# Delta-rule inverses: 32x32 blocks on VectorE, one doubling, substitution with two heads side by side

## The chip, the cores and the metric

The kernel runs on one core of one Trainium2 chip (the other cores are idle). The metric is the device time of one execution in microseconds; it is given as the median of several runs. Five engines work side by side, each through its own queue in order: TensorE (PE) multiplies, VectorE (DVE), ScalarE (ACT) and GpSimd (POOL) do elementwise work, SyncE (SP) issues most of the transfers. Here POOL issues transfers too.

## The reference, cut to what matters

One decoder layer on 256 tokens of width 2048, float32. A combined projection feeds branch A (gated DeltaNet, 8 heads of 128) and branch B (attention, 8 heads); both are gated, projected and added, then a gated MLP follows. The change is in the DeltaNet alone. Per head and chunk the reference computes

```python
a_mat = jnp.where(strict, jnp.einsum('bhncd,bhnsd->bhncs', kb, k) * gamma, 0.0)
t_mat = lax.linalg.triangular_solve(eye + a_mat, eye, left_side=True, lower=True, unit_diagonal=True)
u = jnp.einsum('bhncs,bhnsv->bhncv', t_mat, v * beta[..., None])
...
v_new = u_n - w_n @ state
o = qg_n @ state + qk_n @ v_new
state = state * gl_n + kd_n.T @ v_new
```

`gamma` holds the decays exp(gc[i] - gc[j]) between two tokens of a chunk. The kernel works in chunks of 128 tokens in place of 64, which is the same sum: per head it needs two strictly triangular 128x128 matrices A, the result (I + A)^-1 applied to the values, and the product of the second half's queries and keys with the first half's results.

## The kernel before, in words

**The main work.** Every large product runs as float32 split in a high and a low part, three matmuls of 128x128 by 128x256 for each 128x128 block of weights (`block`, L185 to L190, issued by `main_mm`, L110 to L115). Weights come by SP in 1 MB pieces; ACT rounds each piece to its high part `wh` and DVE subtracts for the low part `wl` (`split`, L120, L118), in halves of 1024 columns and with two buffers of each. The order of the program is: DeltaNet projections (four groups of two heads, each with q, k, v and the output gate z: `ps_gdn`, `ps_z`), attention projections (`ps_moba`, `ps_v`), branch gates (`ps_gate`), branch outputs, `ps_wo`, up (`ps_up`), down (`pd`).

**The background work.** DeltaNet and attention heads are Python generators in the list `bg`. `main_mm` counts 108 (or 215) for each main matmul and calls `tick` after every 1700 (`EVERY`, L29); `tick` advances each generator to its next `yield`, so a piece of background work is written into the program about every 16 main matmuls. `wait(n)` is n empty steps: main work that is put between a transfer and its use. Before the branch gates' tiles are allocated, the generators of the DeltaNet are run out (L702 to L704), since their buffers make room.

**What sets the order.** The program is compiled with a scheduler that runs a timeline model over it and orders each engine's instructions by it, with `tick`'s order as the priority. The order is fixed from then on: an instruction whose input is late holds all that stands behind it on its engine.

**One group's DeltaNet** (`gdn`, L453 to L605; a group is two heads, j, and two halves of 128 tokens, i, so four matrices A). `bc_g`: PE spreads the cumulated decays of a head to 128 partitions with a selecting matmul of their high and low part (L466 to L468). DVE and ACT make `gam` from it (L470 to L477). PE makes the products of keys and queries (`g0`, `g1`), DVE scales them to `aq0`, `aq1` (L506 to L510), which hold A transposed. A goes to DRAM (`dA`, L521, L522) and comes back as 32 diagonal blocks of 16x16, one for each partition (`Xa`, L524). DVE inverts these by 15 pairs of a product and a negated sum (`tm` L530, `X` L531). The blocks go to DRAM and back as `U`, four 128x128 matrices with 16x16 blocks on the diagonal (L537 to L539). Then three levels double the blocks to 32, 64 and 128 (L541 to L568): four transposes `t0`, four matmuls `py` with A, a mask on DVE, four matmuls `pu` with `U`, and a subtraction. With the whole inverse U, `u0` applies it to the first half's values, `r1` takes the first half's part off the second half, `u1` applies the second inverse (L570 to L583). `po` and what follows make the output.

**Queues at the change.** Its transfers are issued by POOL, in order with POOL's own work (squares `sqq` and `so`, rotary products of the attention L636, L637). Weights are issued by SP.

Of the kernel before, what the change touches and what calls it, by code (L numbers as in the profile page):

```python
# [11 lines left out]
F32 = mybir.dt.float32  # L12
F32R = mybir.dt.float32r
# [22 lines left out]
    ("ident", 128), ("nm", 128), ("my", 3 * 64), ("nm3", 3 * 128), ("invf", 1),  # L36
# [3 lines left out]
def const_array():  # L40
    c = {}
    i = np.arange(P)
    c["ident"] = np.eye(P)
    c["nm"] = np.where(i[None, :] >= i[:, None], 0.0, -30000.0)
    my = np.zeros((P, 3, 64))
    for j in range(3):
        m = 16 << j
        e = i[(i // m) % 2 == 0][None, :]
        my[:, j, :] = (i[:, None] // (2 * m) == e // (2 * m)) & ((i[:, None] // m) % 2 == 1)
    c["my"] = my  # L50
# [33 lines left out]
def layer_kernel(ctx: ExitStack, tc: tile.TileContext, xT, pos, cst, csel, ceye, vec, convw, ffw, bdv,  # L84
# [8 lines left out]
    def r3(t, b):  # L93
        return t.rearrange("p (a b) -> p a b", b=b)
# [221 lines left out]
    gch = fk.tile([16, T], F32R, name="gch")  # L316
    gcl = fk.tile([16, T], F32R, name="gcl")
    selr = fk.tile([16, 8, P], F32R, name="selr")
    dve.tensor_copy(selr, self_)
# [68 lines left out]
    def decay():  # L388
# [27 lines left out]
        split(gch, gcl, gc)  # L416
# [11 lines left out]
    def conv4(t, ps, b0):  # L428
# [8 lines left out]
        act.activation(t, t, AF.Silu)  # L437

    zero = fk.tile([P, P], F32, name="zero")
    pool.memset(zero, 0.0)  # L440

    dUs = []
    for i in range(2):
        dUs.append(dr.tile([4, P + 1, P], F32, name=f"dU{i}", bufs=1))

    def diag(d):
        return bass.AP(tensor=d.tensor, offset=d.offset, ap=[[16 * P + 16, 32], [P, 16], [1, 16]])
# [5 lines left out]
    def gdn(h0, kq, v):  # L453
        hs = (h0, h0 + 1)

# [13 lines left out]
        gam = g.tile([P, 2, 3, P], F32, name="gam", bufs=1)  # L469
        for j in range(2):  # L470
            c = 8 + hs[j]
            dve.scalar_tensor_tensor(gam[:, j, 0, :], pg[:, j, :P], cols[:, 0, c:c + 1], nm,
                                     op0=ALU.subtract, op1=ALU.min)
            dve.tensor_scalar(gam[:, j, 1, :], pg[:, j, P:], cols[:, 2, c:c + 1], 0.0, op0=ALU.add, op1=ALU.min)
            dve.scalar_tensor_tensor(gam[:, j, 2, :], pg[:, j, P:], cols[:, 1, c:c + 1], nm,
                                     op0=ALU.subtract, op1=ALU.min)
# [20 lines left out]
        act.activation(st[:, 2, :], st[:, 1, :], AF.Sqrt, bias=epst)  # L497
# [25 lines left out]
        Xa = g.tile([32, 16, 16], F32, name="Xa", bufs=1)  # L523
        pool.dma_start(Xa, diag(dA))  # L524
        X = g.tile([32, 16, 16], F32, name="X", bufs=1)
        pool.tensor_copy(X, eye)
        yield from wait(9)
        for i in range(1, 16):
            tm = g.tile([32, 16, 16], F32, name="tm", bufs=1)
            dve.tensor_tensor(tm[:, :i, :i], X[:, :i, :i], Xa[:, None, :i, i].to_broadcast([32, i, i]), op=ALU.mult)  # L530
            dve.tensor_reduce(X[:, :i, i], tm[:, :i, :i], axis=AX.X, op=ALU.add, negate=True)  # L531
            if i % 4 == 3:
                yield
        dU = dUs[h0 // 2 % 2]
        if h0 < 4:
            sp.dma_start(dU[:, :P].rearrange("p s c -> s p c"), zero[:, None, :].to_broadcast([P, 4, P]))
        pool.dma_start(diag(dU), X)  # L537
        U = g.tile([P, 4, P], F32, name="U0", tag="U", bufs=1)
        pool.dma_start(U, dU[:, :P].rearrange("p s c -> s p c"))  # L539
        yield from wait(12)  # L540
        for lv in range(3):  # L541
            w = 16 << lv

            def even(t):
                return t.rearrange("p a (b c d) -> p a b c d", c=2, d=w)[:, :, :, 0, :]

            def odd(t):
                return t.rearrange("p a (b c d) -> p a b c d", c=2, d=w)[:, :, :, 1, :]

            pst = r3(sdt("t0"), P)  # L550
            for p in range(4):
                pe.transpose(pst[:, p, :], U[:, p, :], ident)
            Tm = g.tile([P, 4, 64], F32, name="Tm", bufs=1)
            act.copy(Tm.rearrange("p a (b d) -> p a b d", d=w), even(pst))
            Y = g.tile([P, 4, P], F32, name="Y", bufs=1)
            pool.memset(odd(Y), 0.0)
            yield
            py = sdt("py")[:, :T].rearrange("p (a b) -> p a b", a=4)
            for p in range(4):
                pe.matmul(py[:, p], ats[p], Tm[:, p], start=True, stop=True)  # L560
            dve.tensor_tensor(even(Y), py.rearrange("p a (b d) -> p a b d", d=w),
                              my[:, lv:lv + 1, :].rearrange("p a (b d) -> p a b d", d=w).to_broadcast([P, 4, 64 // w, w]), op=ALU.mult)
            yield
            pu = sdt("pu")[:, :T].rearrange("p (a b) -> p a b", a=4)
            for p in range(4):
                pe.matmul(pu[:, p], Y[:, p, :], odd(U)[:, p], start=True, stop=True)  # L566
            dve.tensor_tensor(odd(U), odd(U), pu.rearrange("p a (b d) -> p a b d", d=w), op=ALU.subtract)
            yield  # L568
        u = g.tile([P, 4, P], F32, name="u", bufs=1)
        pu0 = r3(sdt("u0"), P)  # L570
        for j in range(2):
            pe.matmul(pu0[:, j, :], U[:, j, :], vb[:, j, :], start=True, stop=True)
        act.copy(u[:, 0:2, :], pu0[:, :2, :])
        yield
        pr = r3(sdt("r1"), P)
        for j in range(2):
            pe.matmul(pr[:, j, :], aq0[:, j, 0, P:], u[:, j, :], start=True, stop=True)
        dve.tensor_tensor(vb[:, 2:4, :], vb[:, 2:4, :], pr[:, :2, :], op=ALU.subtract)
        yield
        pu1 = r3(sdt("u1"), P)  # L580
        for j in range(2):
            pe.matmul(pu1[:, j, :], U[:, 2 + j, :], vb[:, 2 + j, :], start=True, stop=True)
        act.copy(u[:, 2:4, :], pu1[:, :2, :])  # L583
        yield
# [336 lines left out]
```

## Time and profile before

| | us |
|---|---|
| median of 3 runs | 1488.11 (1486.22 to 1488.19) |
| the profiled execution's own time | 1485.81 |
| its span, first to last instruction | 1484.0 |
| PE busy in the span | 1467.9 (99%) |
| DVE busy | 968.6 (65%) |
| ACT busy | 720.1 (49%) |
| POOL busy | 121.9 (8%) |

The DeltaNet's background work lies between about 60 and 410 us of the span; all after that is main work. In the groups and timelines a row names the line, the engine, the operation, output<-input, and the shape as partitions x elements. A float32 matmul appears twice, as two passes; a matmul of split operands and a transpose appear once. The duration of one PE row is longer than its share of PE's time, since matmuls overlap: what one costs is read from start to start.

### The profile page before, as it was taken

To read this page: it belongs to the slowest core of one execution; us is meant where nothing else is said; L and a number is where in the kernel's file an instruction comes from. 1 tells how busy PE (TensorE), PEld (TensorE's weight loads), DVE (VectorE), ACT (ScalarE), POOL (GpSimd) and SP (SyncE) were. 2 spreads that over 40 slices of the span, in tenths; PEclk is the share of its full clock that TensorE was granted. 3 is DMA by queue.
4 is the path that set the end of the run, shared out by engine and by line. 5 is a ranking of instruction groups with operands and counts; after the bars stand their busy time and mean duration, and the time that the engine had idled before them with its cause. 6 is when DMAs were issued, how large, how long until landed. Compare 5 with 4: busy or idle time off the path is not lost.

```text
span 1484.0 us, 26882 instructions
## 1 busy us (share of the span) xinstructions
PE 1467.9 (99%) x11472; PEld 1409.7 (95%) x11472; DVE 968.6 (65%) x1377; ACT 720.1 (49%) x949; POOL 121.9 (8%) x133
## 2 busy tenths in 40 slices
PE   9999999999999999999999999999999999999997
PEld 8999999998999999999999999999999998888886
DVE  7988695887665455766676666666666665445554
ACT  5655363434474344444455454554545554444444
POOL 0001101042121000110100000000000000000000
PEclk9999999999999999999999999999999999999999
DMA  9545544444436555557555555555555554555552
GB/s 335 178 165 180 179 151 161 147 161 155 143 114 226 184 191 195 198 200 277 186 193 199 195 188 191 195 199 199 187 190 194 198 200 170 197 189 189 193 197 86
DMA packets 43353, 277.23 MB, mean 187 GB/s; under 512 B 5248, under 2 KB 6736, under 8 KB 11104
## 3 DMA queue, kind: packets, MB, share of 16 engines
q1 hardware_dynamic: 41408, 270.98, 52.7%
q0 software_dynamic: 960, 2.36, 0.5%
q10 hardware_dynamic: 864, 2.16, 0.4%
q8 instruction: 90, 1.47, 0.4%
q14 instruction: 31, 0.25, 0.0%
HBM read 271.68 MB, written 3.80 MB: 186 GB/s over the span
## 4 chain that ended last, share of the span: by engine, by line
PE 91%; DVE 4%; DMA 2%; issue 1%; ACT 1%; SPq 0%; DVEq 0%; POOLq 0%; ACTq 0%
PE ps_up L111 32%; PE pd L99 16%; PE ps_gate L111 11%; PE ps_gdn L111 8%; PE ps_wo L111 6%; PE ps_br L111 6%; PE ps_moba L111 3%; PE ps_z L111 3%; PE ps_v L111 2%; DVE wl L118 1%; DMA wraw<-in_w_gdn 1%; ACT wh L121 1%; PE py L560 1%; PE g L99 0%; PE pu L566 0%
## 5 line engine op out<-in xcount | busy, mean ns | idle before, releaser
L118 DVE TENSOR_TENSOR wl<-wraw,wh 128x1024 fp32r<-128x1024 f32 (+1 forms) x500 | 605.7, 1248 | 199.7 <-ACT wh L121 199.3
L121 ACT CAST wh<-wraw 128x1024 fp32r<-128x1024 f32 (+1 forms) x500 | 496.1, 1040 | 464.8 <-PE ps_up L111 160.6
L111 PE MATMUL ps_up<-h,wh 128*128 128x256 f32 x2816 | 479.4, 276 | 0.0
L111 PEld LDWEIGHTS ps_up<-h,wh 128*128 128x128 f32 x2816 | 423.7, 188 | 0.1
L111 PE MATMUL ps_up<-h,wl 128*128 128x256 f32 x1408 | 388.9, 276 | 0.0
L111 PEld LDWEIGHTS ps_up<-h,wl 128*128 128x128 f32 x1408 | 264.3, 188 | 0.0
L111 PE MATMUL ps_gate<-hc,wh 128*128 128x256 f32 x1024 | 176.5, 277 | 0.0
L111 PEld LDWEIGHTS ps_gate<-hc,wh 128*128 128x128 f32 x1024 | 154.6, 188 | 0.0
L111 PE MATMUL ps_gate<-hc,wl 128*128 128x256 f32 x512 | 141.8, 277 | 0.4 <-DVE wl L118 0.4
L99 PE MATMUL pd<-wl,ah 128*128 128x512 f32 x336 | 130.9, 390 | 0.0
L99 PE MATMUL pd<-wh,al 128*128 128x512 f32 x336 | 130.8, 389 | 0.0
L111 PE MATMUL ps_gdn<-hc,wh 128*128 128x256 f32 x704 | 124.3, 280 | 0.0
L111 PEld LDWEIGHTS ps_gdn<-hc,wh 128*128 128x128 f32 x704 | 107.1, 188 | 0.8 <-ACT wh L121 0.3
L111 PE MATMUL ps_gdn<-hc,wl 128*128 128x256 f32 x352 | 98.7, 280 | 0.8 <-DVE wl L118 0.8
L111 PEld LDWEIGHTS ps_gate<-hc,wl 128*128 128x128 f32 x512 | 96.1, 188 | 0.6 <-DVE wl L118 0.6
L99 PE MATMUL pd<-wh,ah 128*128 128x512 f32 x336 | 92.8, 391 | 0.0
L111 PE MATMUL ps_moba<-hc,wh 128*128 128x256 f32 x512 | 92.6, 282 | 0.0
L211 DVE TENSOR_TENSOR unf<-ps_up,R 128x512 f32<-128x512 f32 x44 | 30.4, 691 | 88.9 <-PE ps_up L111 88.9
L111 PE MATMUL ps_wo<-mc,wh 128*128 128x256 f32 x512 | 87.1, 276 | 0.0
L111 PEld LDWEIGHTS ps_moba<-hc,wh 128*128 128x128 f32 x512 | 78.4, 189 | 0.2
L111 PEld LDWEIGHTS ps_wo<-mc,wh 128*128 128x128 f32 x512 | 77.2, 188 | 0.0
L121 ACT CAST ah<-acts 128x256 fp32r<-128x256 f32 x44 | 17.9, 407 | 119.2 <-PE pd L99 118.3
(429 smaller groups left out, 2001.9 us busy)
## 6 DMA issues: line engine op xcount, KB each, us to landing
wraw<-in_w_up SPq DMA_DIRECT2D x88, 1024.0 KB, 4.9
wraw<-in_w_dn SPq DMA_DIRECT2D x44, 1024.0 KB, 4.9
wraw<-in_w_gate SPq DMA_DIRECT2D x32, 1024.0 KB, 4.9
wraw<-in_w_gdn SPq DMA_DIRECT2D x30, 1024.0 KB, 4.9
wraw<-in_w_moba SPq DMA_DIRECT2D x16, 1024.0 KB, 4.9
wraw<-in_w_o SPq DMA_DIRECT2D x16, 1024.0 KB, 5.0
wraw<-in_w_mv SPq DMA_DIRECT2D x8, 1024.0 KB, 5.0
wraw<-in_w_ba SPq DMA_DIRECT2D x8, 1024.0 KB, 4.9
```

Of the source, the lines that this page charges most:

```text
L99: pe.matmul(ps, a, b, start=(start and i == 0), stop=(stop and i == n - 1), **kw)
L111: pe.matmul(ps, a, b, start=start, stop=stop, skip_group_check=True)
L118: return (eng or dve).tensor_tensor(lo, src, hi.bitcast(F32), op=ALU.subtract)
L121: act.copy(hi, src)
L211: dve.tensor_tensor(dst, ps, r, op=ALU.mult)
L560: pe.matmul(py[:, p], ats[p], Tm[:, p], start=True, stop=True)
```

## The change

**Decays.** The cumulated decays `gc` go to DRAM once (`dG`) and each group reads its two heads' rows back, spread over 128 partitions, straight into `gam`. The selecting matmuls and the split of `gc` go.

**32x32 inverses on DVE.** A goes to DRAM as before (`dA`). From there its sixteen 32x32 diagonal blocks are gathered (`dC`) and come back so that each block is held by eight partitions (`Xa`); each partition solves two rows of both 16x16 halves, again in 15 pairs of a product and a negated sum (shape 128 x 4 x i). The lower left 16x16 part follows on DVE by two small matrix products (`rows`, which makes `W` and then `Xm`); the second of them needs the lower block's inverse, which goes through DRAM (`dX`, `Xr`). The 32x32 inverses go to DRAM (`dE`), come back as `E`, and are also written on the diagonal of `UB`.

**One doubling for four blocks at once.** `Et` is a transpose of `E` in 32x32 pieces on DVE. One matmul `py` for each half i multiplies four blocks by their part of A (`S1`, block diagonal, read from `dA`); a mask (`Y`); one matmul `pu` for each i; ACT writes the negated result to `UB`.

**Substitution with two heads side by side.** `UB` holds 64x64 inverses of both heads on one diagonal. For each half i: `w0` applies the first, `z0` takes its part (`S2`, also from `dA`) off the values, `w1` applies the second. Values are laid out as two heads x 64 tokens (`v`, `vt`, `vb`, `rt2`); `apart` copies the results back to `u` in the order that `r1` and `po` read. The subtraction behind `r1` is four pieces.

The steps of a generator stay about as many: 47 yields before, 45 now, with other waits (10 before the inverses, 4 and 7 behind them).

**PE, where the first group's inverse is applied.** `t_..`, `py`, `pu` and `u_..` are the levels and the first application; `ps_gdn` is main work. Before, first level and the start of the second, up to the first application:

```order
L552 MATMUL t_1549<-ct,U_1236 128x128 x4
L111 MATMUL ps_gdn<-hc,wl 128x256
...
L560 MATMUL py<-Tm,aq_905 128x64 x2
L560 MATMUL py<-Tm,aq_906 128x64 x2
...
L566 MATMUL pu<-U_1236,Y 128x64 x4
...
L552 MATMUL t_1626<-ct,U_1236 128x128 x4
...
L566 MATMUL pu<-U_1236,Y 128x64 x4
...
L572 MATMUL u_1802<-vb,U_1236 128x128 x2
```

Now, the one doubling and the substitution of the first half:

```order
L563 MATMUL py<-Et,S_387 128x32 x2
L103 MATMUL ps_gdn<-hc,wh 128x256
...
L570 MATMUL pu<-E,Y 128x32 x2
...
L584 MATMUL w_1651<-vb,UB 128x128
...
L590 MATMUL z_1673<-w_1653,S_388 128x128
...
L594 MATMUL w_1712<-vb,UB 128x128
```

What moved: three times four transposes, four `py` and four `pu` have become one time two `py` and two `pu` of 32 columns; the applications of four inverses have become single matmuls, w, z, w for each half. The first of the group's rows (`t` before, `py` now) stands behind 874 main matmuls before and behind 921 now.

**POOL, the first group's transfers, from the matrix A to the inverses.** Before:

```order
L521 DMA dA<-aq_905 128x2x128
L522 DMA dA<-aq_906 128x2x128
L524 DMA Xa<-dA 32x16x16
L537 DMA dU_396<-X 32x16x16
L539 DMA U_1236<-dU_396 128x4x128
L526 COPY X<-eye 32x256
L521 DMA dA<-aq_1513 128x2x128
```

Now:

```order
L506 DMA dA<-aq_902 128x2x128
L441 DMA gam<-dG 128x2x256
L509 DMA dC<-dA 256x1x32 x2
L541 DMA S_388<-dA 64x2x64 x2
L544 DMA S_387<-dA 32x2x32 x4
L511 DMA Xa<-dC 128x1x1024
...
L528 DMA dX<-X 256x1x16
L550 DMA dE<-X 16x8x64
L530 DMA Xr<-dX 128x1x256
L550 DMA dE<-X 16x8x64
L552 DMA E<-dE 128x4x32
L555 DMA UB<-dE 32x2x32 x8
```

What moved: between `dA` and the inverses in place stood `Xa`, `dU`, `U`; now 22 transfers stand there, in a chain dA, dC, Xa, (DVE), dX, Xr, (DVE), dE, E, with the copies of parts of A (`S`) ahead of `Xa` in this group. A group's `gam` is one more. Behind the last row follow the copy that prepares `X` and the second group's `dA`.

The diff, cut to its core:

```diff
@@ decay()
-        split(gch, gcl, gc)
+        pool.dma_start(dG, gc)
@@ gdn()
-        pg = r3(sdt("bc_g"), T)
-        for j in range(2):
-            mmg(pg[:, j, :], [(selr[:, hs[j], :], gch), (selr[:, hs[j], :], gcl)])
+        pool.dma_start(gam[:, :, 0:2, :].rearrange("p j a b -> p j (a b)"), dram(dG, (8 + h0) * T, (0, P), (T, 2), (1, T)))
...
-        act.activation(st[:, 2, :], st[:, 1, :], AF.Sqrt, bias=epst)
+        for j in range(2):
+            for b in range(2):
+                o = slice(64 * b, 64 * b + 64)
+                act.activation(rt2[64 * j:64 * j + 64, :, b], st[o, 1, j::2], AF.Sqrt, bias=epst[o])
...
-        pool.dma_start(Xa, diag(dA))
+        for e in range(2):
+            pool.dma_start(dC[8 * e:8 * e + 8], dram(dA, e * 32 * (P + 1), (64 * (P + 1), 8), (P, 32), (1, 32)))
+        pool.dma_start(Xa[:, :1024], dram(dC, 0, (1024, 16), (0, 8), (1, 1024)))
...
-        yield from wait(9)
+        yield from wait(10)
         for i in range(1, 16):
-            dve.tensor_tensor(tm[:, :i, :i], X[:, :i, :i], Xa[:, None, :i, i].to_broadcast([32, i, i]), op=ALU.mult)
-            dve.tensor_reduce(X[:, :i, i], tm[:, :i, :i], axis=AX.X, op=ALU.add, negate=True)
+            dve.tensor_tensor(tm[:, :, :, :i + 1], Xd[:, :, :, :i + 1],
+                              Ad[:, :, None, :i + 1, i].to_broadcast([P, 2, 2, i + 1]), op=ALU.mult)
+            dve.tensor_reduce(Xd[:, :, :, i], tm[:, :, :, :i + 1], axis=AX.X, op=ALU.add, negate=True)
...
-        pool.dma_start(diag(dU), X)
-        pool.dma_start(U, dU[:, :P].rearrange("p s c -> s p c"))
-        yield from wait(12)
-        for lv in range(3):
...
-            for p in range(4):
-                pe.transpose(pst[:, p, :], U[:, p, :], ident)
...
-            for p in range(4):
-                pe.matmul(py[:, p], ats[p], Tm[:, p], start=True, stop=True)
...
-            for p in range(4):
-                pe.matmul(pu[:, p], Y[:, p, :], odd(U)[:, p], start=True, stop=True)
...
+        pool.dma_start(dX.rearrange("q (a r c) -> (q a) r c", r=2, c=16), X1)
+        pool.dma_start(Xr.rearrange("p m c -> p (m c)"), dram(dX, 0, (256, 16), (0, 8), (1, 256)))
+        rows(W, X0, r3(Xa[:, :512], 32)[:, :, 16:], True)
+        for j in range(2):
+            pool.dma_start(S2[64 * j:64 * j + 64, :, 64 * j:64 * j + 64],
+                           dram(dA, j * (P + 1) * P + 64, (P, 64), (2 * (P + 1) * P, 2), (1, 64)))
+        for q in range(4):
+            pool.dma_start(S1[32 * q:32 * q + 32, :, 32 * q:32 * q + 32],
+                           dram(dA, q * 64 * (P + 1) + 32, (P, 32), (2 * (P + 1) * P, 2), (1, 32)))
+        yield from wait(4)
+        rows(Xm, W, Xr, False)
+        for e in range(2):
+            pool.dma_start(dram(dE, 512 * e, (1024, 16), (64, 8), (1, 64)), X[:, 64 * e:64 * e + 64])
+        pool.dma_start(E.rearrange("p e i c -> p (e i) c"), dram(dE, 0, (32, P), (4096, 4), (1, 32)))
+        for q in range(4):
+            for b in range(2):
+                pool.dma_start(UB[32 * q:32 * q + 32, :, b, 32 * q:32 * q + 32],
+                               dram(dE, q % 2 * 8192 + q // 2 * 2048 + b * 1024, (32, 32), (4096, 2), (1, 32)))
+        yield from wait(7)
+        dve.transpose(Et, E[:, 0])
+        for i in range(2):
+            pe.matmul(py[:, i], S1[:, i], Et[:, i], start=True, stop=True)
...
+        for i in range(2):
+            pe.matmul(pu[:, i], Y[:, i].rearrange("p a b -> p (a b)"), E[:, 1, i], start=True, stop=True)
...
+        for i in range(2):
+            pe.matmul(p0_, UB[:, i, 0], vb[:, i, 0], start=True, stop=True)
+            act.copy(w0, p0_)
+            apart(i, 0, p0_)
+            yield
+            pe.matmul(pz, S2[:, i], w0, start=True, stop=True)
+            dve.tensor_tensor(vb[:, i, 1], vb[:, i, 1], pz, op=ALU.subtract)
+            yield
+            pe.matmul(p1_, UB[:, i, 1], vb[:, i, 1], start=True, stop=True)
+            apart(i, 1, p1_)
```

`S1`, `S2` and `UB` are zeroed once and shared by all groups; `Xa` and `X` have one buffer each, as before.

More of the change, by code (lines that the diff above doesn't have):

```diff
@@ L35 @@
 CONST_FIELDS = [
-    ("ident", 128), ("nm", 128), ("my", 3 * 64), ("nm3", 3 * 128), ("invf", 1),
+    ("ident", 128), ("nm", 128), ("mb", 4 * 32), ("nm3", 3 * 128), ("invf", 1), ("rows", 160),
 ]
@@ L44, in const_array @@
     c["nm"] = np.where(i[None, :] >= i[:, None], 0.0, -30000.0)
[L45 to L50, printed above, removed]
+    c["mb"] = np.kron(np.eye(4), np.ones((32, 32)))
+    rows = np.zeros((16, 8, 2, 80))
+    for r in range(16):
+        rows[:, r // 2, :, r % 2 * 32 + r] = 1.0
+    c["rows"] = rows
     nm3 = np.zeros((P, 3, P))
@@ L315, in layer_kernel @@
     gc = fk.tile([16, T], F32, name="gc")
[L316 to L319, printed above, removed]
     sint = fk.tile([48, T], F32, name="sint")
@@ L436, in conv4, with dram @@
                                          op0=ALU.mult, op1=ALU.add)
[L437 to L447, printed above, removed]
+        if to is None:
+            act.activation(t, t, AF.Silu)
+        else:
+            act.activation(to, t.rearrange("p j (b c) -> p j b c", c=64), AF.Silu)
+    dG = dr.tile([16, T], F32, name="dG", bufs=1)
+    S1 = fk.tile([P, 2, P], F32, name="S1")
+    S2 = fk.tile([P, 2, P], F32, name="S2")
+    UB = fk.tile([P, 2, 2, P], F32, name="UB")
+    for t in (S1, S2, UB):
+        pool.memset(t, 0.0)
+    def dram(t, offset, *ap):
+        return bass.AP(tensor=t.tensor, offset=t.offset + offset, ap=[list(x) for x in ap])
     def wait(n):
@@ new lines, in gdn, with apart @@
+        yield
+        pu = r3(sdt("pu")[:, :64], 32)
+        for i in range(2):
+            pe.matmul(pu[:, i], Y[:, i].rearrange("p a b -> p (a b)"), E[:, 1, i], start=True, stop=True)
+        for j in range(2):
+            for b in range(2):
+                o = 64 * j + 32 * b
+                act.mul(UB[64 * j:64 * j + 32, :, b, 64 * j + 32:64 * j + 64], pu[o:o + 32], -1.0)
+        yield
+        u = g.tile([P, 4, P], F32, name="u", bufs=1)
+        def apart(i, b, pw):
+            for j in range(2):
+                act.copy(u[64 * b:64 * b + 64, 2 * i + j, :], pw[64 * j:64 * j + 64, :])
@@ L565, in gdn @@
-            for p in range(4):
-                pe.matmul(pu[:, p], Y[:, p, :], odd(U)[:, p], start=True, stop=True)
-            dve.tensor_tensor(odd(U), odd(U), pu.rearrange("p a (b d) -> p a b d", d=w), op=ALU.subtract)
+            p1_ = sdt("w1")[:, :P]
+            pe.matmul(p1_, UB[:, i, 1], vb[:, i, 1], start=True, stop=True)
+            apart(i, 1, p1_)
             yield
[L569 to L583, printed above, removed]
@@ L584, in gdn @@
-        yield
+            if i == 0:
+                pr = r3(sdt("r1"), P)
+                for j in range(2):
+                    pe.matmul(pr[:, j, :], aq0[:, j, 0, P:], u[:, j, :], start=True, stop=True)
+                for j in range(2):
+                    for b in range(2):
+                        o = slice(64 * j, 64 * j + 64)
+                        dve.tensor_tensor(vb[o, 1, b], vb[o, 1, b], pr[64 * b:64 * b + 64, j, :], op=ALU.subtract)
+                yield
         po = r3(sdt("po"), P)
@@ L618, in layer_kernel @@
                 ps = chunk(pair(w_gdn, 4 * gr + a), hc, KD, "gdn")
-            conv4(t, ps, 8 * a + h0)
+            if a < 2:
+                conv4(t, ps, 8 * a + h0)
+            else:
+                conv4(t, ps, 8 * a + h0,
+                      v.rearrange("p b (j c) -> p j b c", c=64))
             if gr == 0 and a == 1:
```

93 lines of the change are left out of this document (44 added, 49 removed).

## The prediction

> **What bounds the kernel now.** I read the page's first two parts, then the busy time by stretches, then what PE waits for in the stretch of the DeltaNet (60 to 410 us).
>
> ```profile
> span 1484.0 us, 26882 instructions
> PE 1467.9 (99%) x11472; PEld 1409.7 (95%) x11472; DVE 968.6 (65%) x1377; ACT 720.1 (49%) x949; POOL 121.9 (8%) x133
> PEclk9999999999999999999999999999999999999999
> ```
> ```profile
> core 0: us, PE busy (x) PEld busy (x) DVE busy (x) ACT busy (x) POOL busy (x), PEclk, DMA share, GB/s
> 60.00:320.00 260.00, 258.71 (x2112) 251.96 (x2110) 213.40 (x453) 128.94 (x161) 33.34 (x41) 1.00 0.48 163
> 480.00:1484.00 1004.00, 996.13 (x7727) 953.74 (x7725) 605.20 (x712) 470.93 (x609) 50.57 (x57) 1.00 0.55 192
> ```
> ```profile
> PE pT L662 <- DVE s__3819 L656: 2.0, 1, 2.0
> PE u L582 <- DVE vb L578: 1.6, 1, 1.6
> PE u L572 <- DVE U L567: 1.3, 1, 1.3
> ```
>
> PE is busy 99% at full clock, in the stretch of the change as in the rest. The work behind 480 us is main work that the change does not touch, and 996 of its 1004 us are PE. So time that the change takes from PE's queue comes off the end, and time in which PE stands still because a background result is late is added to it. Nothing else counts directly. The second thing to see is DVE: 213.4 of 260 us busy between 60 and 320 us, 82%. It also makes `wl`, without which the main matmuls stop, so it has 46.6 us to spare there, over four groups. ACT has twice that. The third block shows the only waits of over 1 us that the background causes: three, 4.9 us in all.
>
> **What leaves PE.** A PE row is longer than its share, so I take start to start.
>
> ```profile
> 175.37 0.40 PE L111 MATMUL ps_gdn<-hc,wh 128*128 128x256 f32 x2
> 175.61 0.28 PE L111 MATMUL ps_gdn<-hc,wl 128*128 128x256 f32 x1
> 175.73 0.61 PE L577 MATMUL r<-u,aq 128*128 128x128 f32 x4
> 176.09 0.49 PE L111 MATMUL ps_gdn<-hc,wh 128*128 128x256 f32 x2
> 176.42 0.28 PE L111 MATMUL ps_gdn<-hc,wl 128*128 128x256 f32 x1
> ...
> 200.07 0.60 PE L552 MATMUL t<-ct,U 128*128 128x128 f32 x4
> 200.43 0.49 PE L111 MATMUL ps_gdn<-hc,wh 128*128 128x256 f32 x2
> ...
> 203.59 1.00 PE L560 MATMUL py<-Tm,aq 128*128 128x64 f32 x8
> 204.40 0.48 PE L111 MATMUL ps_gdn<-hc,wh 128*128 128x256 f32 x2
> ```
> ```profile
> 116.05 0.50 PE L462 MATMUL ssq<-ones,sqq 128*128 128x1 f32 x4
> 116.48 0.38 PE L99 MATMUL bc_g<-gch,selr 16*128 16x256 f32 x1
> 117.15 0.50 PE L111 MATMUL ps_gdn<-hc,wh 128*128 128x256 f32 x2
> ...
> 178.91 0.60 PE L582 MATMUL u<-vb,U 128*128 128x128 f32 x4
> 179.35 0.39 PE L588 MATMUL po<-u,aq 128*128 128x128 f32 x2
> ```
>
> A pair of `wh` matmuls takes 0.24 (175.37 to 175.61), and 0.33 right behind an insertion (176.09 to 176.42): every insertion costs 0.09 more than its own interval. So `t` is 200.07 to 200.43 and 0.09, 0.45; `py` 203.59 to 204.40 and 0.09, 0.90; `r` 0.45. A `u` is like `r`, four passes of 128 columns: 0.45 (178.91 to 179.35 gives 0.44). `bc_g` is 116.48 to 117.15, 0.67. `pu` I set equal to `py`, since the groups agree:
>
> ```profile
> L566 PE MATMUL pu<-U,Y 128*128 128x64 f32 x96 | 12.1, 269 | 0.0
> L560 PE MATMUL py<-Tm,aq 128*128 128x64 f32 x96 | 12.0, 268 | 0.0
> ```
>
> A group loses three levels of `t`, `py`, `pu`, 3 x (0.45 + 0.90 + 0.90) = 6.75, two `u`, 0.90, and `bc_g`, 0.67: 8.3. Four groups: **33.3 us off PE**. (96 rows of `py` are four groups, three levels, four matmuls, two passes.)
>
> **What comes onto PE.** A group gains one `py` and one `pu`, each of two matmuls, that is four passes of 32 columns, and six single matmuls of 128 columns (`w` four times, `z` twice), two passes each. Passes of 32 columns are not in the trace; the rows on both sides are `ssq`, four passes of one column, 0.43 (116.05 to 116.48), and `r`, four passes of 128, 0.36. They hardly differ, so width does not set the price there: I take 0.45 with the 0.09, for each of the two. The single ones: half of `r`'s 0.36 and 0.09, 0.27 each, between 0.18 (if nothing behind them slows) and 0.45 (a whole `r`). Sum of a group 0.90 + 1.62 = 2.5, four groups **10.1 us** (8 to 14). Net: **-23.2 us** (-25 to -19).
>
> **Stalls that go.** The two waits at `u` hang on a subtraction that the change removes or splits (2.9 us); `pT` belongs to the attention, which keeps its place. Since what replaces them is again a DVE result between PE instructions (`z`'s subtraction, `r`'s four pieces), I take -2, between 0 and -5.
>
> **DVE.** Rows:
>
> ```profile
> L530 DVE TENSOR_TENSOR tm<-X,Xa 32x1 f32<-32x1 f32 (+14 forms) x60 | 20.8, 346 | 1.8 <-DMA Xa<-dA 0.7
> L531 DVE TENSOR_REDUCE X<-tm 32x1 f32<-32x1 f32 (+14 forms) x60 | 13.5, 225 | 1.0
> L561 DVE TENSOR_TENSOR Y<-py,ct 128x256 f32<-128x256 f32 x12 | 5.0, 416 | 2.8 <-PE py L560 2.8
> L567 DVE TENSOR_TENSOR U<-U,pu 128x256 f32<-128x256 f32 x12 | 4.9, 408 | 3.6 <-PE pu L566 3.6
> L594 DVE TENSOR_REDUCE st<-so 128x4 f32<-128x512 f32 x4 | 2.7, 686 | 7.0 <-POOL so L593 7.0
> L530 DVE TENSOR_TENSOR tm<-X,Xa 32x64 f32<-32x64 f32 x4 | 1.0, 254 | 0.1
> L531 DVE TENSOR_REDUCE X<-tm 32x8 f32<-32x64 f32 x4 | 0.8, 207 | 0.1
> ```
>
> Per group the change removes (20.8 + 13.5 + 5.0 + 4.9)/4 = 11.05 us. It adds 15 pairs of at most 64 elements per partition, at most 0.254 + 0.207 each: I take 0.40, 6.0 us. `W` and `Xm` are two operations of 512 elements each, by the `st` row 4 x 0.69 = 2.8. `Y` is 0.42 as before; `z`'s two subtractions 0.3 each, `Et` 0.2, and the four pieces behind `r` cost some 0.8 more than the one before (a DVE row of few elements takes 0.2 to 0.25, so the price is in the count). Together 10.8: DVE's work is **even**. ACT gets more, smaller pieces (`apart` eight, UB four, two `w0`, against three `Tm` and two `u`), some 3 us a group by 0.3 each, beside the half of its time that is free. What hides both is that share of idle time; without it, at worst, their difference of ±3 us per group would be on the path.
>
> **The chain of transfers, which replaces the three levels.** This is the part on which the sign hangs. The first `t` now starts here, and its inputs and POOL's transfers take:
>
> ```profile
> 88.64 0.87 DVE L509 SCALAR_TENSOR_TENSOR aq<-g,st,gam 128x256 f32<-128x256 f32 x2
> 133.83 0.61 PE L552 MATMUL t<-ct,U 128*128 128x128 f32 x4
> ```
> ```profile
> dA<-aq POOLq DMA_DIRECT2D x8, 128.0 KB, 2.2
> Xa<-dA POOLq DMA_DIRECT2D x4, 32.0 KB, 4.7
> dU<-X POOLq DMA_DIRECT2D x4, 32.0 KB, 3.7
> U<-dU POOLq DMA_DIRECT2D x4, 256.0 KB, 5.4
> ```
> ```profile
> L524 POOL DMA_DIRECT2D Xa<-dA x4 | 2.7, 681 | 8.0 <-DMA dA<-aq 6.0 <-issue 2.0
> ```
>
> `aq` is done at 89.5. By the order, `py` of the change stands behind 921 main matmuls where `t` stood behind 874: 47 x 0.12 (0.24 a pair) = 5.6 later, less the `bc_g` and the other things removed ahead of it, 1.3: about 138.0. That leaves 48.5 us. What must fit in: `gam` now comes by DMA and makes `aq` later by up to one hop (3.5); `dA` with its issue 3.0; `dC`, `Xa`, `dX`, `Xr`, `dE`, `E`, six hops of 32 KB to 64 KB, each an issue of 0.7 (the POOL row: 681 ns) and a landing time L, with one more issue of 0.7 wherever a transfer comes in two halves, and with the six `S` transfers, 4.2, standing ahead of `Xa` on POOL's queue; on DVE 15 pairs, which share it with the `wl` of 1.25 us each, about 15 us, and `W`, `Xm`, `Et` 3.0. With L = 2.2, the shortest of the four rows, this is 3.5 + 3.0 + 6 x 2.9 + 1.4 + 18 = 43.3 and some 4 for `S`, where it isn't hidden behind `dC`: between 5.2 and 1.2 us to spare. With L = 4.7, `Xa`'s, it is 15 us more: 10 to 14 too late. The pairs are shared with `wl` only until DVE has nothing else, and the landing times are medians under weight loads which do not all coincide, so I set the hop at the middle, L = 3.3 (as `dU`, the write of small pieces, less the part that issue already counts): about 2 us late in the first group. Other groups have 52 to 58 us by the same count of main matmuls and are not late. In all I take **+4 us** of new waits, from 0 to 20.
>
> [...]
>
> **The sum.** -23.2 - 2 + 4 = -21. On the profiled execution's own 1485.8 (span 1484.0 and 1.8 around it) that is 1464.6. It lies 2.3 below the median of 1488.1, so against the median: **1467 us**.
>
> **Rivals.**
>
> *DVE's queue becomes the bound.* The DeltaNet's stretch shrinks by some 20 us, with DVE's work unchanged: 213 of about 240, 88%, with 27 to 30 us free. An instruction that waits for a transfer holds all the `wl` behind it, and there are now four of them per group (`gam`, `Xa`, `Xr`, `E`) where there were two. If each held DVE 2.5 us, that is 40 us against some 29 idle: 11 of the 21 go, and the time is about **1477**. For it: `Xa` was already waited for once (0.7 in its row). Against it: the waits written into the program (10, 4 and 7 steps) let `wl` pass ahead.
>
> *Slower: the hops of small pieces.* If they land in 5.4 us, as `U` does, a group's chain takes 43.3 + 4 + 6 x 3.2 = 66.5. The four groups have about 54 on average (48.5 and three of 52 to 58), so each would be about 12 late, and `py` then holds PE's whole queue, main work included: 12 x 4 = 48, less the 25 gained, +23, **1511**. It decides from about 6 us of lateness per group, that is from L near 4.4. For it: the `Xa` and `U` rows. Against it: `dA`, written in 512-byte pieces, needs 2.2 and `dU` 3.7, and `U` moves four to eight times as much as a hop of the new chain.
>
> *No change.* The lateness may just eat the gain: 5 to 7 us per group (L of 4.2 to 4.6), **1488**; or the main work's weights may be what sets the pace once PE is faster (the DMA share of 0.48 and ACT at half say no).
>
> **How the numbers follow.** 0.2% is 3 us, about what a measurement of this kernel can tell from none. The forecast, a gain of 12 to 31 us, has 0.65; its own range is 1457 to 1476 (low: -25 of PE, -5 of stalls, nothing late; high: -19 with lateness of 7). DVE as the bound 0.17, slower by the hops 0.12, no change 0.06. The first two are faster: 0.82. The range takes the forecast's and DVE's cases and the nearer part of the loss of gain, 1457 to 1484; above it lie no change and slower, 0.18.
>
> **What would show it.** Right: some 11264 PE rows (288 off, 80 on); `py` and `pu` with four passes of about 0.4 from start to start; fewer than 5 us of PE waits on `py`, `w`, `z`, `u`; the front's main work ending some 20 us earlier with 480 us and later unchanged in length. The landing times of `dC`, `Xa`, `dX`, `Xr`, `dE` and `E` decide between forecast and rivals: below 3.5 the first, above 4.4 the slower one. Waits of `wl` behind `Xa`, `Xr` or `E` on DVE, followed by PE waits for `wl`, would show DVE as the bound. The forecast is wrong if `py` waits over 6 us per group, or if a single matmul between main work costs twice the 0.27.

## The result and the profile after

The changed kernel took 1470.85 us (median of 4 runs, 1470.02 to 1472.34) beside 1487.58 for the kernel before: a ratio of 0.989, 95% interval 0.9873 to 0.9907, 16.7 us faster. On another occasion (run e12 below) the same kernel took 1474.51, ratio 0.9904 (0.9889 to 0.9919). So variants that differ by less than about 4 us can't be told apart here.

The changed kernel's page, first lines, and its busy time by stretches (columns as in the prediction's table; the bounds lie where the same main work begins and ends as in the stretches of before, some 15 us earlier):

```profile
span 1468.7 us, 26659 instructions
PE 1445.5 (98%) x11264; PEld 1387.4 (94%) x11264; DVE 971.6 (66%) x1395; ACT 727.1 (50%) x994; POOL 171.9 (12%) x208
```
```profile
60.00:305.00 245.00, 237.01 (x1899) 230.04 (x1898) 214.30 (x469) 136.98 (x198) 74.32 (x110) 0.99 0.56 184
465.00:1468.00 1003.00, 995.62 (x7722) 953.25 (x7721) 604.86 (x712) 470.77 (x609) 50.75 (x57) 1.00 0.56 192
```

The 11264 PE rows are there, and the last 1003 us are as long as before: the whole difference lies in the DeltaNet's stretch. PE has lost 22.4 us of busy time, but in that stretch it now stands still for 8 of 245 us where it did for 1.3 of 260, and the clock is no longer 1.00 throughout. DVE's work is the same (214.3 and 213.4) in a stretch that is 15 us shorter.

PE's own waits in the front (line, whom it waited for: us, times, longest):

```profile
PE pot L624 <- DVE ot L619: 3.8, 2, 2.0
PE w L584 <- DVE vb L604: 2.9, 1, 2.9
PE ps_gdn L103 <- DVE wl L110: 1.1, 2, 0.8
PE ps_moba L103 <- DVE wl L110: 0.9, 1, 0.9
PE ps_v L103 <- DVE wl L110: 0.8, 1, 0.8
...
PE py L563 <- issue: 0.6, 1, 0.6
```

The place on which the sign hung, `py` behind the chain of transfers, cost 0.6 us once, and there no transfer came last: `E` was issued at 133.86 and there some 2.4 us later, but `Et`, which `py` reads, began at 137.39 without idle time before it, behind four `aq` in DVE's queue. The stalls are elsewhere, at `pot` (transpose of the output) and `w`, and all of them but this name DVE. The waits for `wl` are 2.8 us in four; before there was one, of 0.4.

**The longer stall at `pot`, followed back.** DVE, PE and POOL around 180 us (start, duration, what; in brackets the idle time before and what ended it), and TensorE's clock behind it (two stretches of 3.41 us; first PE's busy time, and the clock is the column after the busy times):

```profile
177.04 0.18 DVE L618 RECIPROCAL st<-st 128x4 f32<-128x4 f32 x1 [0.27 <-ACT st L617]
181.41 1.02 DVE L534 TENSOR_TENSOR tw<-W,Xr 128x512 f32<-128x512 f32 x1 [4.20 <-DMA Xr<-dX]
182.34 0.69 DVE L619 TENSOR_TENSOR ot<-ot,st 128x512 f32<-128x512 f32 x1
```
```profile
183.18 0.63 PE L624 MATMUL pot<-ct,ot 128*128 128x128 f32 x4 [2.04 <-DVE ot L619]
```
```profile
171.44 0.69 POOL L528 DMA_DIRECT2D dX<-X  x1 [5.35 <-DVE X L523]
172.04 0.64 POOL L550 DMA_DIRECT2D dE<-X  x1
172.59 1.15 POOL L614 TENSOR_TENSOR so<-ot 128x512 f32<-128x512 f32 x1
176.22 0.56 POOL L530 DMA_DIRECT2D Xr<-dX  x1 [2.48 <-DMA dX<-X]
```
```profile
181.71:185.12 3.41, 1.95 (x15) 1.88 (x16) 3.41 (x5) 0.00 (x0) 0.55 (x1) 1.00 0.02 6
185.12:188.53 3.41, 3.41 (x14) 3.02 (x13) 3.41 (x10) 0.00 (x0) 2.29 (x4) 0.50 0.52 141
```

`dX` leaves at 171.4, `Xr` can be issued at 176.2 and is there at 181.4. From 177.2 to 181.4 DVE holds still for it, although `ot` of the group before, next in its queue, has all its inputs at 177.2. PE reaches `pot` at 181.1 and waits 2.04 us for `ot`. Two microseconds after the stall the granted clock falls to a half for 3.4 us; that takes another 1.7 us. The `Xr` wait is thus a loss for work that has nothing to do with it. The second stall at `pot` (1.73 us, at 312 us) has no wait for `Xr` before it: there DVE had stood 2.19 us for GpSimd's `so`, and its `tw`, without a wait, took 2.13 us in place of 1.02.

DVE's waits for transfers in the front:

```profile
DVE tw L534 <- DMA Xr<-dX: 7.6, 3, 4.2
DVE gam L454 <- DMA gam<-dG: 1.0, 2, 0.7
DVE Et L559 <- DMA E<-dE: 0.9, 1, 0.9
```

**The stall at `w`** in the fourth group has other causes. DVE and POOL:

```profile
277.14 0.68 DVE L660 TENSOR_TENSOR rt<-qk,sint 16x512 f32<-16x512 f32 x1 [2.36 <-POOL qk L663]
...
278.77 0.18 DVE L523 TENSOR_REDUCE X<-tm 128x4 f32<-128x20 f32 x1
278.99 0.98 DVE L521 TENSOR_TENSOR tm<-X,Xa 128x24 f32<-128x24 f32 x1
280.00 0.18 DVE L523 TENSOR_REDUCE X<-tm 128x4 f32<-128x24 f32 x1
280.22 1.09 DVE L521 TENSOR_TENSOR tm<-X,Xa 128x28 f32<-128x28 f32 x1
...
282.46 1.19 DVE L604 TENSOR_TENSOR vb<-vb,r 64x128 f32<-64x128 f32 x4
```
```profile
278.59 1.31 POOL L662 TENSOR_TENSOR qk<-qk,cost 48x512 f32<-48x512 f32 x1 [1.49 <-DVE rt L661]
279.98 1.27 POOL L663 TENSOR_TENSOR qk<-qk,rt 48x512 f32<-48x512 f32 x1
```

DVE first stands 2.36 us for GpSimd's `qk` (the attention's rotary sum). Then small products of 128 x 24 and 128 x 28, which take 0.2 us elsewhere, take 1.0 and 1.1 while GpSimd multiplies and adds, and the four pieces of `r`'s subtraction take 1.19 where one took 0.41. That is 2.4, 1.7 and 0.8 us, together more than the 2.86 us that `w` stood; how the stall is shared among them isn't shown. Behind this one too the clock fell, for the same 1.7 us.

**The sum.** A table in which each profiled execution is split. "PE waits" is the idle time that the timeline of PE shows between 60 and 460 us, "clock" the sum of (1 - granted clock) over stretches of 1 us there, and "rest" what is left of the span. (Labels are those of the experiments.)

| | span | PE waits | clock | rest |
|---|---|---|---|---|
| before | 1484.0 | 5.3 | 0 | 1478.7 |
| changed | 1468.7 | 11.3 | 3.4 | 1454.0 |
| e1, no wait for Xr | 1459.9 | 6.4 | 0 | 1453.5 |
| e2, one more hop ahead of E | 1465.9 | 8.4 | 1.7 | 1455.8 |
| e3, 6 empty steps | 1469.4 | 12.5 | 0 | 1456.9 |
| e4, before with decays by DMA | 1480.2 | 4.3 | 1.7 | 1474.2 |
| e5, no wait for Xr and E | 1457.2 | 3.6 | 0 | 1453.6 |
| e6, r in one piece | 1464.1 | 8.0 | 3.4 | 1452.7 |
| e7, 8 empty steps | 1471.1 | 12.9 | 3.4 | 1454.8 |
| e9, second product on GpSimd | 1479.3 | 16.4 | 6.8 | 1456.1 |
| e10, one more hop ahead of Xr | 1466.7 | 9.2 | 1.7 | 1455.8 |
| e11, both hops | 1476.5 | 15.3 | 3.4 | 1457.8 |
| e12, changed kernel again | 1473.8 | 12.6 | 3.4 | 1457.8 |

All kernels with the new inverses have a rest of 1453 to 1458 (e12 stood 2.0 us for its first input, before 60 us, and lost 1.7 of clock behind that). Most of what differs between them, 1457 to 1479 in the span, is waits and clock. These are single executions, so differences of a few us between the rows carry little.

### The profile page after: what moved, and what is told of

Same layout as the page of the kernel before. It is cut to its first block, busy times and chain, and to the rows that moved or that the text cites. A ratio compares the mean times of both kernels' runs of the same rounds, so it can differ in the third digit from the quotient of the medians.

```text
span 1468.7 us, 26659 instructions
## 1 busy us (share of the span) xinstructions
PE 1445.5 (98%) x11264; PEld 1387.4 (94%) x11264; DVE 971.6 (66%) x1395; ACT 727.1 (50%) x994; POOL 171.9 (12%) x208
## 4 chain that ended last, share of the span: by engine, by line
PE 86%; DVE 6%; DMA 3%; ACT 2%; issue 2%; POOL 1%; SPq 0%; DVEq 0%; POOLq 0%; ACTq 0%
PE ps_up L103 33%; PE pd L91 16%; PE ps_gate L103 12%; PE ps_wo L103 6%; PE ps_br L103 6%; PE ps_gdn L103 4%; PE ps_moba L103 3%; PE ps_v L103 2%; DVE wl L110 2%; PE ps_z L103 2%; DMA wraw<-in_w_gdn 1%; DMA Xr<-dX 1%; ACT wh L113 1%; DMA dX<-X 1%; DVE tm L521 1%
## 5 line engine op out<-in xcount | busy, mean ns | idle before, releaser
L816 POOL TENSOR_TENSOR acts<-sg,cvf 128x256 f32<-128x256 f32 x44 | 32.4, 737 | 459.4 <-ACT sg L815 459.4
```

The lines of the kernel that those rows point to most:

```text
L816: pool.tensor_tensor(acts[:, c, :], sg, t[:, 1, :], op=ALU.mult)
```

## The experiments

**Theory A:** VectorE's queue, held by a wait for a transfer, makes unrelated work late for TensorE. **Theory B:** VectorE is full and the losses would come in one form or another; or the chain's length itself is the price.

**e1: the wait for Xr left out.**

```diff
+    K0 = r3(ct[:, 256:512], 16)
-        rows(Xm, W, Xr, False)
+        rows(Xm, W, K0, False)
```

> The changed kernel, but the second small product on VectorE (the one that makes Xm) reads a constant instead of Xr; the transfers dX and Xr stay, nothing waits for them, and Xm is therefore not the reference's. Theory A (VectorE's queue is held by the wait for Xr, 7.6 us in three waits, and the work queued behind it, ot above all, reaches TensorE late): the stall of 2.04 us at the output transpose and the lower clock behind it (1.7 us) go, and with them some of the waits for wl: 1464 to 1467 us against 1470.9. Theory B (VectorE is simply full in this stretch and another wait takes the place): 1469 to 1471 us.

Measured 1462.65 (1461.69 to 1464.01), ratio 0.9839 (0.9825 to 0.9852): 8 us below the changed kernel of the first occasion, beyond what theory A gave. The stall at `pot` in the second group and every lowered clock are gone; of PE's waits the largest left is one of 3.43 us at the second `w` (line 596 there), behind DVE's backlog in the fourth group:

```profile
PE w L596 <- DVE vb L593: 3.4, 1, 3.4
```

So the wait for `Xr` is worth about half of what PE loses. It is one wait of DVE's queue, not work: DVE's instructions are as many as before. The order made at compile time hardly moved: `py` of the four groups stands behind 921, 1315, 1685 and 2081 main matmuls, against 921, 1296, 1690 and 2094 in the changed kernel.

**e5: also no wait for E.**

```diff
-        dve.transpose(Et, E[:, 0])
+        EK = C["mb"].rearrange("p (e i c) -> p e i c", e=2, i=2)
+        dve.transpose(Et, EK[:, 0])
-            pe.matmul(pu[:, i], Y[:, i].rearrange("p a b -> p (a b)"), E[:, 1, i], start=True, stop=True)
+            pe.matmul(pu[:, i], Y[:, i].rearrange("p a b -> p (a b)"), EK[:, 1, i], start=True, stop=True)
```

> As the run that leaves the wait for Xr out, and also Et and the second factor of pu read a constant in place of E, so that neither VectorE nor TensorE waits for the end of the chain (UB still does); the results are not the reference's. If the chain's lateness at py is worth what the trace shows (0.6 us once on TensorE, 0.9 us on VectorE), this is within 1 us of the run without the wait for Xr: 1464 to 1467 us. If E's lateness is the larger loss, 1460 to 1463 us.

Measured 1458.88 (1457.90 to 1459.14), ratio 0.9807 (0.9794 to 0.9821): 4 us less than e1, the larger of the two expectations. The trace of the changed kernel showed 1.5 us of such waits. The order, made anew at compile time, also places `py` of the first group earlier (behind 848 main matmuls where the changed kernel has 921), so the 4 us are those of a kernel planned without that wait and not of the wait alone. PE's waits are down to 3.6, less than before the change; the largest of them is one of 1.6 for `wl`. Without the chain's two waits, and in that order, the gain is 27.9 us.

**e2, e10, e11: the chain made longer.** A copy within DRAM ahead of `E` (e2), ahead of `Xr` (e10), and both (e11).

```diff
+        dE2 = dr.tile([16, 32, 32], F32, name="dE2")
+        pool.dma_start(dE2, dE)
+        dE = dE2
         E = g.tile([P, 2, 2, 32], F32, name="E", bufs=1)
```

> The changed kernel with one more transfer in the chain: dE is copied within DRAM before E and UB read it, so each group's chain is one issue and one landing (about 0.7 + 4.2 us) longer. Theory A (the chain is just in time in every group: E is waited for 0.9 us in one and py stood 0.6 us in another): each of the four groups is late by some 3 to 5 us, 12 to 20 us in all plus lost clock: 1483 to 1495 us. Theory B (only the first group is tight, the later ones have 4 us and more to spare, as the prediction had it): 1473 to 1477 us.

> The changed kernel with one more transfer between dX and Xr (dX is copied within DRAM), about 5 us more in each group ahead of the instruction on VectorE that waits for Xr. If the order made at compile time allows for a transfer by less than it takes, the wait for Xr on VectorE grows from 7.6 us by what is missing, four times: with 2 us missing to about 15 us, and the time to 1473 to 1480 us. If the order allows for the whole, the wait stays at 6 to 9 us and py stands some 30 to 40 main matmuls later, as with the additional transfer behind dE: 1468 to 1472 us.

> The changed kernel with both additional transfers, dX copied within DRAM ahead of Xr and dE copied ahead of E: about 10 us more of chain in each group. Theory A (what costs is a transfer that comes later than the fixed order allows, not the chain's length; each additional transfer moves its users back by more than it takes): as fast as with one, 1467 to 1470 us, with waits on VectorE for Xr and E of under 5 us together. Theory B (the chain's length itself costs as soon as the room is used): slower than the changed kernel, 1474 us and more.

Measured: e2 1469.34 (1467.66 to 1470.26; ratio 0.9868 to 0.9895), e10 1469.16 (1468.49 to 1469.59; 0.9864 to 0.9894), e11 1477.44 (1473.04 to 1480.74; 0.9905 to 0.9944). One more transfer in the chain costs nothing that can be measured, against my expectation of 12 to 20 us for e2: `py` of the first group simply stands further back, behind 952 (e2) and 1029 (e10) main matmuls in place of 921 (in e10 by 108, where I had expected 30 to 40), and DVE waits less for `Xr` than in the changed kernel, in e2 and e10:

```profile
DVE tw L534 <- DMA Xr<-dX: 4.3, 3, 1.6
```
```profile
DVE tw L537 <- DMA Xr<-dX: 3.6, 2, 2.9
```

So with one transfer more the chain's length didn't set the price here: there was main work to put beside it. With both hops the waits come back (7.7 us for `Xr`, 15.3 of PE waits); both are what theory B expected. But the changed kernel itself took 1474.51 on the same chip (e12), and the intervals overlap, so whether two hops cost is left open.

**e12: the changed kernel again.**

> The changed kernel itself, beside the run with two additional transfers on the same chip, so that differences of one or two us between the variants can be read against it: 1470 to 1472 us.

Measured 1474.51 (1472.54 to 1476.37), 2.5 to 4.5 us above the expectation. Its profiled execution has the same stalls at the same places; the one at `pot` is 2.62 us instead of 2.04, and the half clock behind it lasted twice as long (3.4 us lost).

**e3 and e7: more empty steps between Xr's issue and its use**, 6 and 8 in place of 4.

```diff
-        yield from wait(4)
+        yield from wait(6)
         rows(Xm, W, Xr, False)
```

> The changed kernel with 6 empty steps in place of 4 between Xr's issue and its use (some 3.4 us more main work in between); the rest of the chain moves back by as much. Theory A (the wait for Xr on VectorE is the loss): the waits of 7.6 us for Xr shrink to under 2, and the time goes to 1465 to 1468 us. Theory B (the loss moves along: later steps collide with the attention's work on VectorE): 1470 to 1474 us.

> The changed kernel with 8 empty steps in place of 4 between Xr's issue and its use. If the wait for Xr is the loss and 6 steps hide it, 8 give no more: as with 6, within 1.5 us. If the later steps collide with the attention's work on VectorE, 8 are slower than 6 by 1 to 4 us.

Measured 1470.83 (1469.65 to 1473.44) and 1472.51 (1470.68 to 1473.80): no gain from either. With 6 steps the edit didn't do what I meant: `py` of the first three groups stands where it stood (921, 1296 and 1690 main matmuls), and DVE still waits 6.7 us for `Xr`. With 8 steps that wait does shrink, to 1.6, but others take its place, on DVE in e7:

```profile
DVE st L615 <- POOL so L614: 5.9, 2, 4.1
...
DVE Et L559 <- DMA E<-dE: 3.3, 1, 3.3
DVE tw L534 <- DMA Xr<-dX: 1.6, 2, 1.1
```

Theory B's form: the loss moved along the chain.

**e9: the second product on GpSimd**, so that DVE never waits for `Xr`.

```diff
-        rows(Xm, W, Xr, False)
+        tp = g.tile([P, 2, 16, 16], F32, name="tp", tag="sq", bufs=1)
+        pool.tensor_tensor(tp, W[:, :, None, :].to_broadcast([P, 2, 16, 16]),
+                           Xr.rearrange("p m c -> p c m")[:, None].to_broadcast([P, 2, 16, 16]), op=ALU.mult)
+        for n_ in (8, 4, 2):
+            pool.tensor_tensor(tp[:, :, :, :n_], tp[:, :, :, :n_], tp[:, :, :, n_:2 * n_], op=ALU.add)
+        pool.tensor_tensor(Xm, tp[:, :, :, 0], tp[:, :, :, 1], op=ALU.add)
```

> The changed kernel with the second small product (Xm from W and Xr) on GpSimd, as one product and four additions in place of a product and a sum on VectorE; it computes the same. VectorE then never waits for Xr (7.6 us) and loses 4 x 1.7 us of work; GpSimd needs some 4 us per group in its place, so E is later by some 2 us. Theory A (the wait of VectorE's queue for Xr was the loss): 1463 to 1467 us. Theory B (the end of the chain sets py, and later is worse; or GpSimd's elementwise work slows VectorE): 1471 to 1476 us.

Measured 1481.82 (1479.75 to 1484.29), ratio 0.9966 (0.9953 to 0.9978): slower than the changed kernel by 7 to 11 us, more than theory B gave. The wait for `Xr` is off DVE, as meant, and the next wait of the chain takes its place. DVE's wait, PE's wait, and GpSimd's groups (busy us, mean ns):

```profile
DVE Et L564 <- DMA E<-dE: 9.0, 3, 6.8
```
```profile
PE py L568 <- DVE st L450: 3.3, 1, 3.3
```
```profile
L551 POOL TENSOR_TENSOR tp<-tp 128x256 f32<-128x256 f32 (+2 forms) x12 | 10.4, 868 | 0.9
L548 POOL TENSOR_TENSOR tp<-W,Xr 128x512 f32<-128x512 f32 x4 | 6.7, 1668 | 10.6 <-DMA Xr<-dX 6.8 <-DVE st L623 1.9 <-DVE s__3485 L678 1.8
```

On GpSimd the product and its additions take some 5 us per group (6.7 + 10.4 + 2.7 over four), against 1.7 on DVE, and `E` comes later; DVE, held by it for up to 6.8 us, is late with work for which PE then stands at `py`. Here the prediction's second rival, a chain too late for `py`, is what happens in one group. It is 3.3 of PE's 16.4 us of waits; the rest stands at other places, with 6.8 us of clock lost behind the stalls.

**e4: the decays alone**, on the kernel before: `dG`, `gam` by transfer, no `bc_g` (the edit is the change's own).

> The kernel before with the decays spread by DMA as in the change, and nothing else of it. By the prediction's term for bc_g, 4 x 0.67 = 2.7 us come off TensorE: 1485 us against 1487.6. Rival: gam's transfer stands in POOL's queue and VectorE waits for it, which eats the 2.7 us: 1487 to 1489 us.

Measured 1481.88 (1481.05 to 1483.14), ratio 0.9967 (0.9955 to 0.9980): 4.9 us faster, so the decays are a quarter or more of the whole gain, and more than the 2.7 that I gave them. In the traces `bc_g` from start to start is 2.85 us, and 0.4 more for the slower pairs behind it; another 0.6 comes before 60 us, where one load fewer stands ahead of the weights. The rest of the 4.5 in the table is not accounted for.

**e6: r's subtraction in one piece.**

```diff
-                for j in range(2):
-                    for b in range(2):
-                        o = slice(64 * j, 64 * j + 64)
-                        dve.tensor_tensor(vb[o, 1, b], vb[o, 1, b], pr[64 * b:64 * b + 64, j, :], op=ALU.subtract)
+                dve.tensor_tensor(vb[:, 1], vb[:, 1], pr[:, :2, :], op=ALU.subtract)
```

> The changed kernel with the subtraction behind r1 as one instruction of 128 x 256 in place of four pieces of 64 x 128 (0.41 against 1.19 us on VectorE); it takes the values in another order, so the result is not the reference's. Theory A (the stall of 2.86 us at w in the fourth group is VectorE's backlog: its small pairs took 1.0 us in place of 0.2 while GpSimd's rotary products ran): 1 us or less saved, 1469.5 to 1471 us. Theory B (the four pieces make w late): the stall and its lost clock go, 4.5 us: 1466 to 1467 us.

The one instruction takes the values in another order than the four pieces. Measured 1466.81 (1465.84 to 1472.18), ratio 0.9855 to 0.9891, which overlaps the changed kernel's. The five executions lie in two bunches, three up to 1466.81 and two at 1471.52 and 1472.18; only one of the first was profiled. In it the stall at the fourth group's `w` is gone, but waits of 2.44 and 4.91 us for `wl` stand in its place and the clock loss is the same 3.4. DVE's wait of 2.36 us for GpSimd's `qk` is gone as well, since the order is another, so the run doesn't tell the causes of that stall apart. Theory B's number came out without its mechanism; I count it as undecided. The wait of 4.91 us shows the first mechanism once more, DVE and then PE:

```profile
298.52 1.02 DVE L534 TENSOR_TENSOR tw<-W,Xr 128x512 f32<-128x512 f32 x1 [5.45 <-DMA Xr<-dX]
```
```profile
301.98 0.58 PE L103 MATMUL ps_moba<-hc,wl 128*128 128x256 f32 x1 [4.91 <-DVE wl L110]
```

DVE stands 5.45 us for `Xr`, and the `wl` behind it in its queue (300.71 to 301.92) comes that much later: the sign that the prediction had given for its first rival.

**e8: the clock behind a pause, by itself.** Behind the end of the changed kernel, three times twelve blocks of 40 matmuls with growing pauses.

```diff
+    for rep in range(3):
+        for m_ in range(1, 13):
+            for _ in range(40):
+                pe.matmul(pd[0][0], pr_, hh[:, :512], start=True, stop=True, skip_group_check=True)
+            dve.tensor_scalar(pr_, pd[0][0][:, :P], 0.0, None, op0=ALU.mult)
+            for _ in range(m_):
+                dve.tensor_scalar(pr_, pr_, 0.5, None, op0=ALU.mult)
```

> The changed kernel with a piece behind its end: three times twelve blocks of 40 matmuls of 128 x 512, with pauses between them that grow from about 0.8 to about 5 us (a chain of 1 to 12 VectorE instructions that the next block reads). It measures the granted clock behind a pause by itself. If the two stalls of 2.0 and 2.9 us in the changed kernel are what lowered the clock: blocks behind pauses of 2 us and more show a stretch at half clock, those behind pauses below 1.7 us don't. If it has to be longer than 3.4 us (as the changed kernel's stalls weren't), only the longest pauses show it.

Two neighbouring blocks, and the stretch at the start of the second one (the clock is the column of 0.50):

```profile
1514.01 9.60 PE L884 MATMUL pd<-tail,prb 128*128 128x512 f32 x40 [1.69 <-DVE prb L887]
1525.56 11.15 PE L884 MATMUL pd<-tail,prb 128*128 128x512 f32 x40 [1.95 <-DVE prb L887]
```
```profile
1526.00:1529.00 3.00, 3.00 (x8) 2.33 (x8) 0.00 (x0) 0.00 (x0) 0.00 (x0) 0.50 0.00 0
```

Pauses of up to 1.69 us were followed by full speed in all three rounds; 1.95 by half speed in one of three; 2.21 and every longer one by half speed each time, for 3.4 us (for 6.8 behind those of 3.26 us); a block of 9.60 us then took 10.9 to 11.2 (12.2 behind 3.26). The first expectation holds.

## Why the prediction was right, and where it was off

It said 1467, range 1457 to 1484, a gain of 21. Measured: 1470.85, a gain of 16.7. By its terms:

- **PE's work, -23.2.** Right. The table's rest fell by 24.7 (1478.7 to 1454.0). The decays had 2.7 in it and are 4.5 in e4's rest; the inverses had 20.5 and are 20.2. The single insertions, from the changed kernel's timeline of PE:

```profile
142.02 0.53 PE L570 MATMUL pu<-E,Y 128*128 128x32 f32 x4
142.38 0.36 PE L103 MATMUL ps_gdn<-hc,wh 128*128 128x256 f32 x1
...
146.14 0.38 PE L584 MATMUL w<-vb,UB 128*128 128x128 f32 x2
146.28 0.48 PE L103 MATMUL ps_gdn<-hc,wh 128*128 128x256 f32 x2
146.60 0.28 PE L103 MATMUL ps_gdn<-hc,wl 128*128 128x256 f32 x1
```

  Four passes of 32 columns take 0.36, like four of 128 in `r`: the choice between the two bounds was right. A `w` is 0.14 and 0.08 for the slower pair, 0.22 where I had 0.27.
- **Waits, -2 and +4.** The sum of +2 was mis-sized: it is +6.0, and +3.4 of lowered clock with it, 9.4 in all. For the lowered clock the sum had no term. That is the whole of the miss: -24.7 + 9.4 = -15.3 in the span, where the sum had -21.
- **Where the waits are.** The step that failed is "the chain of transfers", which had PE wait at `py` in the first group. The chain was even slower than assumed. Its transfers in the changed kernel (KB each, median us to landing):

```profile
Xa<-dC POOLq DMA_DIRECT2D x4, 512.0 KB, 5.6
...
Xr<-dX POOLq DMA_DIRECT2D x4, 128.0 KB, 3.8
...
dC<-dA POOLq DMA_DIRECT2D x8, 32.0 KB, 5.2
...
dE<-X POOLq DMA_DIRECT2D x8, 32.0 KB, 2.2
E<-dE POOLq DMA_DIRECT2D x4, 64.0 KB, 4.2
...
dX<-X POOLq DMA_DIRECT2D x4, 16.0 KB, 3.2
```

  They are 4.0 on average where I had 3.3 (and `Xa` and `Xr`, in eight copies, are 512 and 128 KB, not the 32 to 64 that I wrote, in pieces of 4 and 1 KB by their access patterns). The mean lies between the marks of 3.5 and 4.4 that I had set. By my own sum `py` would have been some 10 us late. It was late by 0.6, because several terms that I added lie beside others: `gam` cost `aq` nothing (done at 89.28, 89.51 before), the six `S` transfers are issued while `dC` lands, and `W` and one half of `dE` lie beside `dX`. What it did wait for was DVE's queue. `py` was issued at 137.7, where I had 138.0.
- **The lateness showed one engine earlier**, as in the first rival: an instruction of DVE that waits for a transfer (`Xr`, 7.6 us) holds what is queued behind it. I gave that rival 0.17 and 11 us of gain; what came lies between it and the forecast. Its sign, PE waiting for `wl`, is 2.8 of the 11.3 us; the larger waits are for `ot` and `vb`, held in the same queue. e1 shows that this wait is worth about 8 us, e9 and e7 that it can't be moved off by itself without the next one of the chain coming late.
- **The rival with slow hops** did not come true in the change (e2: a hop more costs nothing), but one group of e9 is a case of it.
- **DVE's work even:** right, 214.3 for 213.4 in the stretch. (ACT had 131 us to spare there, nearly three times DVE's 46.6, not twice; nothing hung on it.)

No variant that computes the same is clearly faster than the changed kernel: e2 and e10 are 1 to 2 us below it, less than its own two occasions differ.

## What to carry to other kernels

Here a chain of small transfers replaced work of a full engine, and the price was paid where an engine working through its queue in order waited for a link of the chain (7.6 us of DVE for `Xr`; without that wait the kernel took 8 us less). So list what stands behind each such instruction (here `ot` and `wl` behind `Xr`), not only the last user. The compile-time order made room for one more transfer on its own (e2 1469.34 and e10 1469.16 against 1470.85); moving a single wait uncovered the next one (e7, e9). And the saving itself can be counted well from start-to-start intervals, to within 2 us of 25 here.

## What I had not expected

A stall of TensorE can cost more than its length: in the changed kernel the granted clock fell to a half for 3.41 us, 1.7 us lost, behind stalls of 2.04 and 2.86 us. In the kernel before, stalls of 1.29, 1.60 and 2.00 had no such effect; stalls of 2.84 and 3.43 in e3 and e1 went without it. The traces show what goes with it: where an execution has several falls of the granted clock, they lie on a grid of 3.41 us (the changed kernel's two, at 185.12 and 284.11 us, are 29 steps apart; the eighteen in e8's probe, e9's three and e11's two lie whole steps apart too), and a fall goes with how long TensorE stood within the one step before it. That was 1.5 us (3.41 less 1.95 busy, in the lines at `pot` above) and 2.8 in the changed kernel. e1's 3.43 us lie across a boundary, 1.61 on one side and 1.82 on the other:

```profile
277.23:280.64 3.41, 1.80 (x16) 1.59 (x14) 3.27 (x7) 0.21 (x1) 2.27 (x3) 1.00 0.87 286
280.64:284.05 3.41, 1.59 (x13) 1.59 (x14) 3.41 (x7) 0.52 (x2) 1.45 (x2) 1.00 0.12 41
```

In e12 a stall of 2.87 us went without it too, with 1.73 and 1.14 in the two steps. In the probe of e8 and between 21 and 478 us of e9 to e12, by the idle times that the timeline of PE shows, all 25 steps at full clock with 1.90 us or more of idle TensorE were followed by half clock, and none of those with 1.77 us or less. The 1.5 us in the changed kernel don't fit that, nor does e4, which lost 1.7 us of clock although its longest stall was 1.5; why is open. Otherwise, in these runs, a stall of 2 to 3.4 us was followed by half clock or not by where it fell on the grid.

A DVE product of 128 x 24 took 1.0 us in place of 0.2 while GpSimd worked on 48 x 512, and ended at 279.97, just behind GpSimd's instruction (279.90). Whether the two share something, or what, was not tested.
